# Gated-delta scan: heads in pairs, two pairs half a step apart, with the Fourier output projection as filler

## Chip, cores and metric

One core of one Trainium2 chip. The metric is the device time of one execution in microseconds, lower is better.

## The reference

One encoder layer on 1024 tokens (plus 16 meta tokens) of width 1024, in float32. A combined projection of the normed input gives a Fourier branch, q, k, v of eight heads, an output gate z and two branch gates. Each head runs a gated delta rule in chunks of 64 tokens, once forwards and once backwards; a mixture of experts follows.

```python
def step(state, inp):
    q_c, k_c, u_c, w_c, qk_c, dec_c = inp
    v_new = u_c - einsum("bhcd,bhdv->bhcv", w_c, state)
    o_c = einsum("bhcd,bhdv->bhcv", q_c, state) + einsum("bhcs,bhsv->bhcv", qk_c, v_new)
    state = state * dec_c[..., None, None] + einsum("bhcd,bhcv->bhdv", k_c, v_new)
    return state, o_c
...
o = rms_norm(o_fwd + o_bwd, out_norm_g) * silu(zf)
y_d = o @ w_delta
y_f = real(fft2(f_in)) @ w_fourier
merged = sigmoid(gate_f) * y_f + sigmoid(gate_d) * y_d
return merged @ w_out
```

## The kernel before

Stages follow each other on the core: norm and heads (projections of q, k, v, their convolution, and the inverses of the triangular matrices, on the vector engine in pool `ip`), `middle`, `scan`, `delta` (the product with w_delta), `output`, experts. Matmuls of 128 x 512 are made of three products of high and low parts (`mm3_g`, and L220 in `product`), with the split of the operands in `split` (high part on ScalarE, L860, low part on VectorE, L861).

A gate tile is `project_gate` for one of eight column tiles of a kind (0: z, 1: gate of the Fourier branch, 2: gate of the delta branch): 48 matmuls of 128 x 512 at L220, an activation to `zt` (L1689), and stores to `dz` in DRAM. `middle` computes the Fourier transform, gate kind 1, then `fourier_out` for eight tiles (24 matmuls each by `mm3`, L867, then a product with the gate, `gt`, stored to `dmf`), with three tiles of kind 0 between them (ZB). The other thirteen gate tiles are `filling()`, a generator that `fill(ns)` advances by so many ns of matmuls.

`scan` runs eight heads, 16 steps each, both directions at once: the forward chunk stands in partitions 0 to 63, the backward one in 64 to 127. Two heads are under way at a time, four ticks apart. A `scan_step` has: state (four matmuls, L739), R (VectorE, L741), the scaled q part `so` (L744 on ScalarE for t < 8, L746 on VectorE after), T (L748), vd and vn (ScalarE, L750, L752), dS (two matmuls, L757), S (VectorE, L758), Q (L760), the add to `so` (L761), and from t = 8 the squares. Order on TensorE is that of the code in `scan` (`manual_schedule`); the other engines are ordered by the tile scheduler. Loads of a head (`skq`, `svtok`, `sktok`) go over SP for heads 0 and 1, over POOL for the others, T and Q likewise. `scan_out` and `scan_put` norm a head's output, transpose it (L782), multiply with z and store it to `don` as 512 KB over POOL. The PSUM pools are pmain (3), pds (1), pmisc (1), pproj2 (2). Behind the scan stand the puts left over, the rest of the filler, and `delta`, which loads `don`, `dmf` and `dz`. What `fill` and its constants are:

```python
LEAD = 22e3
FILL = 90e3
SHARE = (0.1, 0.2, 0.1, 0.2, 0.2, 0.2)
```

## Time and profile before

| | us |
|---|---|
| median of 3 runs | 1860.27 (1860.0 to 1862.33) |
| profiled execution | 1857.15 |
| its span | 1855.3 |
| last matmul of `middle` starts | 721.08 |
| first state of the scan | 753.04 |
| last step of the scan, about | 1099 |
| first matmul of `delta` | 1122.13 |

The mean granted clock of the profiled execution is 0.966 of full speed. A row of PE's timeline gives the start of a run of like matmuls, the time until the last of them ends, and their number; since matmuls are pipelined, the distance of two starts tells what a group takes, not its length. One float32 matmul shows as two in the counts of the scan's lines.

### The profile page before, as it was taken

The numbers are of one execution on the slowest core, as the hardware profiler recorded it, in microseconds if no ns is written. First come the engines' busy times: TensorE is split into PE (matmuls) and PEld (weight loads), VectorE is DVE, ScalarE is ACT, GpSimd is POOL, SyncE is SP. The second block draws the span as 40 slices with busy tenths as digits, with TensorE's granted clock in tenths as the row PEclk, the third lists the DMA queues.
The fourth block names the chain that finished last, engine by engine and source line by source line (L and its number), as shares of the span: only waits on it lengthen the run. The fifth ranks groups of instructions, "written<-read, shape, count | busy, mean of one in ns | idle before, by whom it ended". The sixth has DMA issues, their size and how long they took to land. (4 is left out here: it accounts for less than half of the span.)

```text
span 1855.3 us, 26469 instructions
## 1 busy us (share of the span) xinstructions
PE 1730.6 (93%) x10018; PEld 1241.1 (67%) x10018; DVE 1043.3 (56%) x2195; ACT 696.9 (38%) x1539; POOL 188.4 (10%) x297
## 2 busy tenths in 40 slices
PE   7978989889999999799999999999699999999996
PEld 6968888878978887566666677888544443443342
DVE  6645558777955898456556555632634344424433
ACT  5645546444432211444444443421133232323231
POOL 2000001000010001023223100000100111001000
PEclk9998999988999999899999999999899999999998
DMA  4143542334466346734434337735499999999995
GB/s 156 51 124 114 159 137 93 101 105 134 137 198 179 122 158 206 193 106 137 146 114 128 101 117 246 224 98 216 143 402 418 419 419 419 420 419 419 420 419 204
DMA packets 149613, 395.35 MB, mean 213 GB/s; under 512 B 68151, under 2 KB 70367, under 8 KB 124511
## 3 DMA queue, kind: packets, MB, share of 16 engines
q1 hardware_dynamic: 132744, 337.65, 49.3%
q0 software_dynamic: 15248, 55.21, 9.2%
q8 instruction: 81, 1.33, 0.3%
q10 hardware_dynamic: 1488, 0.73, 0.2%
q14 instruction: 52, 0.43, 0.1%
HBM read 330.38 MB, written 65.26 MB: 213 GB/s over the span
## 5 line engine op out<-in xcount | busy, mean ns | idle before, releaser
L220 PE MATMUL proj<-xh,wh 128*128 128x346 f32 (+5 forms) x1080 | 395.9, 367 | 12.1 <-ACT pad L356 6.2
L220 PE MATMUL proj<-xl,wh 128*128 128x346 f32 (+4 forms) x1080 | 395.6, 366 | 0.0
L220 PE MATMUL proj<-xh,wl 128*128 128x346 f32 (+4 forms) x1080 | 394.0, 366 | 0.0
L220 PEld LDWEIGHTS proj<-xh,wh 128*128 128x128 f32 (+1 forms) x1080 | 208.2, 193 | 33.2 <-ACT pad L356 7.0
L220 PEld LDWEIGHTS proj<-xl,wh 128*128 128x128 f32 (+1 forms) x1080 | 208.1, 193 | 18.7 <-issue 5.8
L220 PEld LDWEIGHTS proj<-xh,wl 128*128 128x128 f32 (+1 forms) x1080 | 207.3, 192 | 19.3 <-issue 6.7
L373 DVE SCALAR_TENSOR_TENSOR acc<-pad,convw,acc 128x520 f32<-128x520 f32 x192 | 136.2, 752 | 22.2 <-ACT acc L369 22.1
L860 ACT ACTIVATE wh<-wr 128x1024 fp32r<-128x1024 f32 (+2 forms) x77 | 77.2, 1004 | 132.1 <-PE proj L220 68.2
L1336 DVE SCALAR_TENSOR_TENSOR ea<-ea,gw,gu 128x256 f32<-128x256 f32 x32 | 15.4, 480 | 176.3 <-ACT ea L1335 176.3
L861 DVE TENSOR_TENSOR wl<-wr,wh 128x1024 fp32r<-128x1024 f32 (+2 forms) x77 | 88.8, 1154 | 40.9 <-ACT wh L860 40.7
L688 DVE TENSOR_TENSOR tmp<-M 128x62 f32<-128x62 f32 (+30 forms) x124 | 105.9, 854 | 7.2 <-DMA M<-dL 5.6
L690 DVE TENSOR_TENSOR M<-M,tmp 128x62 f32<-128x62 f32 (+30 forms) x124 | 105.9, 854 | 1.8
L741 DVE SCALAR_TENSOR_TENSOR R<-main,egn,svtok 128x128 f32<-128x128 f32 x128 | 44.8, 350 | 101.6 <-PE main L739 101.5
L750 ACT ACTIVATE vd<-main,vdec 128x128 f32<-128x128 f32 x128 | 46.9, 366 | 137.0 <-PE main L748 136.8
L758 DVE SCALAR_TENSOR_TENSOR S<-S,egl,dS 128x128 f32<-128x128 f32 x240 | 72.6, 342 | 39.5 <-PE dS L757 39.1
L739 PE MATMUL main<-S,skq 128*64 128x128 f32 x1024 | 86.1, 288 | 0.1
L1335 ACT ACTIVATE ea<-gu 128x256 f32<-128x256 f32 x32 | 12.3, 384 | 187.3 <-PE gu L1331 187.3
L1361 DVE TENSOR_TENSOR yl<-dn,yh 128x512 fp32r<-128x512 f32 x64 | 44.1, 689 | 60.1 <-ACT yh L1360 60.1
L739 PEld LDWEIGHTS main<-S,skq 128*64 128x64 f32 x1024 | 54.7, 137 | 31.0 <-DVE so L761 16.9
L1360 ACT ACTIVATE yh<-dn 128x512 fp32r<-128x512 f32 x64 | 38.1, 595 | 97.8 <-PE dn L1358 97.2
L1331 PE MATMUL gu<-ml,gx 128*64 128x512 f32 x288 | 68.7, 594 | 3.0 <-DMA ml<-in_w_gu_dram 3.0
L1331 PE MATMUL gu<-mh,gx 128*64 128x512 f32 x288 | 67.0, 593 | 1.5 <-DMA mh<-in_w_gu_dram 1.5
(430 smaller groups left out, 3161.7 us busy)
## 6 DMA issues: line engine op xcount, KB each, us to landing
mh<-in_w_gu_dram SPq DMA_DIRECT2D x36, 1024.0 KB
ml<-in_w_gu_dram SPq DMA_DIRECT2D x36, 1024.0 KB
wr<-in_w_t_dram SPq DMA_DIRECT2D x52, 512.0 KB
wx<-in_w_gu_dram SPq DMA_DIRECT2D x20, 1024.0 KB
mh<-in_w_dn_dram SPq DMA_DIRECT2D x20, 1024.0 KB
ml<-in_w_dn_dram SPq DMA_DIRECT2D x18, 1024.0 KB
yh<-in_w_gu_dram SPq DMA_DIRECT2D x16, 1024.0 KB
yl<-in_w_gu_dram SPq DMA_DIRECT2D x16, 1024.0 KB
```

What stands on the lines that cost most here:

```text
L220: nc.tensor.matmul(o, w[:, k, :n], x[:, k, a:b], start=(m == 0), stop=(m == 23))
L373: nc.vector.scalar_tensor_tensor(o, pad[:, a + j:a + j + NT // 2], w[:, j:j + 1], o, op0=OP.mult, op1=OP.add)
L688: nc.vector.tensor_tensor(tv, M[:, j + 1:, j:j + 1].to_broadcast([np_, m, j]), M[:, j:j + 1, :j].to_broadcast([np_, m, j]), op=OP.mult)
L690: nc.vector.tensor_tensor(M[:, j + 1:, :j], M[:, j + 1:, :j], tv, op=OP.add)
L739: nc.tensor.matmul(ps[hs[half], i], kv[:, i, 2 * (p % 4) + half], st[half], start=True, stop=True)
L741: nc.vector.scalar_tensor_tensor(R, ps[:, 0], self.egn[:, col:col + 1], d["vtok"][p // 4][:, p % 4], op0=OP.mult, op1=OP.add)
L750: nc.scalar.activation(vd, ps[:, 2], AF.Copy, scale=self.vdec[:, col:col + 1])
L758: nc.vector.scalar_tensor_tensor(st[half], st[half], self.egl[:, half, col:col + 1], dS, op0=OP.mult, op1=OP.add)
L860: self.nc.scalar.activation(hi, src, AF.Copy)
L861: self.nc.vector.tensor_tensor(lo, src, hi.bitcast(F32), op=OP.subtract)
L1331: nc.tensor.matmul(pg[self.HS[i]], d["x"][:, 4 * kk + k, c:c + 64], w[:, 4 * i + k], start=(kk == 0 and k == 0), stop=(kk == 1 and k == 3))
L1361: nc.vector.tensor_tensor(yl[:, cs], pd, yh[:, cs].bitcast(F32), op=OP.subtract)
```

## The change

Heads go in pairs P = 0 to 3, and two pairs (lanes) run half a step apart: in half-step u one lane does its state and its solve (T), the other, of which the step began in the half-step before, its update (dS, S) and its output (Q). PSUM tiles hold two heads; T and Q have a bank each (pTQ), pmain is pM with 2 buffers, the transposes share pproj2 with the filler. For t of 8 and more the scaled q part goes from ScalarE to `oq` and is added on POOL. The output is put in two halves per pair, at t = 11 and t = 15; loads of z and stores of `don` are on SP, 64 stores of 128 KB. T and Q come in blocks of four steps on SP, loads of a pair on SP (first half of the first two pairs) or POOL. All 24 gate tiles stand in `middle`; `fourier_out` is the filler, and its inputs yh, yl, its weights and the scan's right-hand tiles lie where the normed input and the weight tiles were until the middle's end (`hx.close()`).

```diff
-            for _ in self.project_gate(1):
-                pass
-            with tc.tile_pool(name="wf", bufs=2) as tp:
-                yh, yl = self.load_y(tp, self.dy, 4)
-                for dt in range(8):
-                    self.fourier_out(tp, pf, dt, yh, yl)
-                    if dt < self.ZB:
-                        for _ in self.project_gate(0, dt, dt + 1):
-                            pass
+            for kind in (1, 0, 2):
+                for _ in self.project_gate(kind):
+                    pass
...
+        d["o"] = sc.tile([128, 8, 2, 128], F32, name="so", bufs=3)
+        d["ss"] = sc.tile([128, 8, 2], F32, name="oss", bufs=3)
...
+    def pair_load(self, d, b, eng):
+        for i in range(2):
+            h = 2 * d["P"] + i
             ps = slice(4 * b, 4 * b + 4)
+            eng.dma_start(d["kq"][i, b], self.dkq[h][:, :, 512 * b:512 * b + 512])
+            eng.dma_start(d["vtok"][i, b], self.dv[h][:, ps])
+            eng.dma_start(d["ktok"][i, b], self.dk[h][:, ps])
...
+            T, Q = self.slots[d["lane"], i, k % 2]
+            for half in range(2):
+                hs = self.HALVES[half]
+                n0 = 64 * (half ^ v) + 32 * half + 8 * (h % 4) + 4 * b
+                eng.dma_start(T[hs, :, hs], self.dT[h // 4][n0:n0 + 4].rearrange("p s c -> s p c"))
+                eng.dma_start(Q[hs, :, hs], self.dQK[h][hs, v, 4 * b:4 * b + 4])
...
+        ps = self.pM.tile([128, 2, 2, 128], F32, name="main")
+        for i in range(2):
+            kv = d["kq"][i, p // 4].rearrange("c k (s t) -> c k s t", t=64)
+            for j in range(2):
+                for half in range(2):
+                    nc.tensor.matmul(ps[self.HALVES[half], j, i], kv[:, j, 2 * (p % 4) + half],
+                                     d["S"][i][0 if half == v else 1], start=True, stop=True)
+        d["R"] = R = self.sc.tile([128, 2, 128], F32, name="R")
+        for i in range(2):
+            nc.vector.scalar_tensor_tensor(R[:, i], ps[:, 0, i], self.egn[:, cols[i]:cols[i] + 1],
+                                           d["vtok"][i, p // 4][:, p % 4], op0=OP.mult, op1=OP.add)
+        o = d["o"][:, p] if v == 0 else self.sc.tile([128, 2, 128], F32, name="oq")
+        for i in range(2):
+            nc.scalar.activation(o[:, i], ps[:, 1, i], AF.Copy, scale=self.eg[:, cols[i]:cols[i] + 1])
+        if v == 1:
+            nc.gpsimd.tensor_tensor(d["o"][:, p], d["o"][:, p], o, op=OP.add)
...
+        ps = self.pTQ.tile([128, 2, 128], F32, name="psT")
+        for i in range(2):
+            nc.tensor.matmul(ps[:, i], mats[i][0][:, p % 4], d["R"][:, i], start=True, stop=True)
+        d["vd"] = vd = self.sc.tile([128, 2, 128], F32, name="vd")
+        d["vn"] = vn = self.sc.tile([128, 2, 128], F32, name="vn")
+        for o, c in ((vd, self.vdec), (vn, self.beta)):
+            for i in range(2):
+                nc.scalar.activation(o[:, i], ps[:, i], AF.Copy, scale=c[:, cols[i]:cols[i] + 1])
...
+        dS = [self.pds.tile([128, 2, 128], F32, name=f"dS{half}") for half in range(2)]
         for i in range(2):
             for half in range(2):
+                hs = self.HALVES[half]
+                nc.tensor.matmul(dS[half][:, i], d["ktok"][i, p // 4][hs, p % 4], d["vd"][hs, i], start=True, stop=True)
...
+        ps = self.pTQ.tile([128, 2, 128], F32, name="psQ")
+        for i in range(2):
+            nc.tensor.matmul(ps[:, i], mats[i][1][:, p % 4], d["vn"][:, i], start=True, stop=True)
         o = d["o"][:, p]
+        nc.vector.tensor_tensor(o, o, ps, op=OP.add)
+        if v == 1:
+            for i in range(2):
+                sq = self.sc.tile([128, 128], F32, name="osq", bufs=1)
+                nc.scalar.activation(sq, o[:, i], AF.Square, accum_out=d["ss"][:, p, i:i + 1])
...
+    def pair_put(self, d, b, eng):
+        nc, sc, P = self.nc, self.sc, d["P"]
+        ps4 = slice(4 * b, 4 * b + 4)
+        o = d["o"][:, ps4]
+        zs = []
+        for i in range(2):
+            z = sc.tile([128, 8, 64], F32, name="oz")
+            for k, c in ((0, 4 * b), (4, 12 - 4 * b)):
+                nc.sync.dma_start(z[:, k:k + 4].rearrange("p n t -> p (n t)"), self.dz[0, :, 2 * P + i, 64 * c:64 * c + 256])
+            zs.append(z)
+        x = sc.tile([128, 4, 2], F32, name="ox")
+        nc.vector.scalar_tensor_tensor(x, d["ss"][:, ps4], 1.0 / 128.0,
+                                       self.epsq[:, 2 * P:2 * P + 2, ps4].rearrange("c h p -> c p h"), op0=OP.mult, op1=OP.add)
+        r = rsqrt_of(nc, sc, x, [128, 4, 2], "or")
+        eng.tensor_tensor(o, o, r[:, :, :, None].to_broadcast([128, 4, 2, 128]), op=OP.mult)
         yield
+        for i in range(2):
+            yield
+            ps = self.pproj.tile([128, 512], F32, name="proj")
             for j in range(4):
+                nc.tensor.transpose(ps[:, 128 * j:128 * j + 128], o[:, j, i], self.ident)
             pv = ps.rearrange("p (n a t) -> p n a t", a=2, t=64)
+            z = zs[i]
+            for a, zz in ((0, z[:, 0:4]), (1, z[:, 7:3:-1])):
                 nc.vector.scalar_tensor_tensor(zz, pv[:, :, a], self.ong, zz, op0=OP.mult, op1=OP.mult)
+            for k, c in ((0, 4 * b), (4, 12 - 4 * b)):
+                nc.sync.dma_start(self.don[:, 2 * P + i, 64 * c:64 * c + 256], z[:, k:k + 4].rearrange("p n t -> p (n t)"))
...
+        lanes = []
+        for lane in range(2):
+            d = self.pair(lane)
+            self.pair_load(d, 0, nc.sync)
+            self.pair_mats(d, 0, nc.sync)
+            self.pair_start(d)
+            lanes.append(d)
+        yh, yl = self.load_y(self.fin, self.dy, 4)
+        self.filler = self.fourier_out(yh, yl)
+        for d in lanes:
+            self.pair_load(d, 1, nc.gpsimd)
+            self.pair_mats(d, 1, nc.sync)
         self.fill(self.LEAD)
+        nxt, puts = {}, []
+        prev = None
+        for u in range(65):
+            lane, n = u % 2, u // 2
+            now = None
+            if n < 32:
+                t = n % 16
+                if n == 16:
+                    lanes[lane] = nxt.pop(lane)
+                    self.pair_start(lanes[lane])
+                now = lanes[lane], t
+                self.step_state(*now)
+            if prev is not None and prev[1] < 15:
+                self.step_update(*prev)
+            self.fill(self.FILL / 64)
+            if now is not None:
+                self.step_solve(*now)
+            if prev is not None:
+                self.step_out(*prev)
+                d, t = prev
+                if t in (11, 15):
+                    b = 1 if t == 11 else 0
+                    puts.append(self.pair_put(d, b, nc.vector if d["P"] > 1 and b == 0 else nc.gpsimd))
+                if t % 4 == 3:
+                    k = t // 4 + 2
+                    if k < 4:
+                        self.pair_mats(d, k, nc.sync)
+                    elif d["P"] < 2:
+                        if k == 4:
+                            nxt[d["lane"]] = e = self.pair(d["P"] + 2)
+                            self.pair_load(e, 0, nc.gpsimd)
+                        else:
+                            self.pair_load(nxt_of(nxt, lanes, d), 1, nc.gpsimd)
+                        self.pair_mats(nxt_of(nxt, lanes, d), k - 4, nc.sync)
+            for g in list(puts):
+                if next(g, 1):
+                    puts.remove(g)
+            prev = now
+        while puts:
+            self.fill(self.TAIL / 6)
+            for g in list(puts):
+                if next(g, 1):
+                    puts.remove(g)
+        self.fill(1e9)
+    LEAD = 10e3
+    FILL = 26e3
+    TAIL = 6e3
...
-            hx = ExitStack()
+            cx, hx = ExitStack(), ExitStack()
...
             self.middle()
+            hx.close()
             self.pproj = en(tc.tile_pool(name="pproj2", bufs=2, space=PSUM))
-            self.zp = enx(tc.tile_pool(name="zp", bufs=2, side="right"))
-            self.filler = self.filling()
...
-                self.sc = ens(tc.tile_pool(name="sc", bufs=3, side="right"))
-                self.pmisc = ens(tc.tile_pool(name="pmisc", bufs=1, space=PSUM))
+                self.fin = ens(tc.tile_pool(name="fin", bufs=1, side="right"))
+                self.fw = ens(tc.tile_pool(name="fw", bufs=2, side="right"))
+                self.sc = ens(tc.tile_pool(name="sc", bufs=2, side="right"))
...
-                    self.slp = en2(tc.tile_pool(name="sl", bufs=4))
-                    self.pmain = en2(tc.tile_pool(name="pmain", bufs=3, space=PSUM))
+                    self.slp = en2(tc.tile_pool(name="sl", bufs=8))
+                    self.pM = en2(tc.tile_pool(name="pM", bufs=2, space=PSUM))
+                    self.pTQ = en2(tc.tile_pool(name="pTQ", bufs=1, space=PSUM))
                     self.pds = en2(tc.tile_pool(name="pds", bufs=1, space=PSUM))
...
-                    for h in data:
-                        for _ in self.scan_put(h, data[h]):
-                            pass
-                    self.fill(1e9)
                     sx.close()
-                    hx.close()
+                    cx.close()
...
+        yh = tp.tile([128, kt, S], F32R, name="yh")
+        yl = tp.tile([128, kt, S], F32R, name="yl")
...
+    def fourier_out(self, yh, yl):
+        nc, fw = self.nc, self.fw
+        for dt in range(8):
+            wh, wl = (fw.tile([128, 4, 128], F32R, name=n) for n in ("fwh", "fwl"))
+            wr = fw.tile([128, 4, 128], F32, name="fwr")
+            nc.sync.dma_start(wr, self.io["w_fou"][dt])
+            self.split(wh, wl, wr)
+            for c in range(2):
+                ts = slice(512 * c, 512 * c + 512)
+                ps = self.pproj.tile([128, 512], F32, name="proj")
+                g = fw.tile([128, 512], F32, name="gt")
+                nc.sync.dma_start(g, self.dz[1, :, dt, ts])
+                for n, x in enumerate(self.mm3_g(ps, lambda k: wh[:, k], lambda k: wl[:, k],
+                                                 lambda k: yh[:, k, ts], lambda k: yl[:, k, ts], 4)):
+                    if n == 11:
+                        nc.vector.tensor_tensor(g, g, ps, op=OP.mult)
+                        nc.sync.dma_start(self.dmf[:, dt, ts], g)
+                    yield x
```

On PE, a stretch of the steady scan before, one head-step and a bit (proj is the filler; main<-S the state, dS the update, main<-vn the output, main<-R the solve):

```order
L739 MATMUL main<-S_7335,skq 64x128
L739 MATMUL main<-S_7334,skq 64x128
...
L220 MATMUL proj<-xh,wl 128x512
L757 MATMUL dS_8125<-vd,sktok 128x128
L757 MATMUL dS_8128<-vd,sktok 128x128
L760 MATMUL main<-vn,Q_6579 128x128
L220 MATMUL proj<-xh,wh 128x512
L748 MATMUL main<-R,T_6574 128x128
L739 MATMUL main<-S_7572,skq 64x128
```

The same place after, one half-step of two heads:

```order
L750 MATMUL main<-S_7088,skq 64x128
...
L750 MATMUL main<-S_7093,skq 64x128
L781 MATMUL dS_7677<-vd,sktok 128x128
L781 MATMUL dS_7678<-vd,sktok 128x128
...
L920 MATMUL proj<-yl,fwh 128x512
L767 MATMUL psT<-R,m_7052 128x128
L767 MATMUL psT<-R,m_7054 128x128
L793 MATMUL psQ<-vn,m_7056 128x128
```

The filler that stood between state and update, and between output and solve, is gone from there; one place for it is left, ahead of the solve.

On SP after, between the middle and the scan's first steps (yr is the Fourier branch to be split, skq, svtok, sktok the first pair loads; L711 to L713 stand four times):

```order
L1747 DMA dz<-zt 128x512 [waits DMAHW5_49,Activation_49]
L1718 DMA yr<-dy 128x1024 [waits DMAHW6_49,DVE_49,PE_49]
L1727 DMA fwr<-in_w_fou_dram 128x512 [waits DMAHW7_49]
...
L711 DMA skq<-dkq 128x2x512 [waits DMASW7_49,DMASW6_49,DMAHW0_49,DMASW5_49,DMAHW7_49,DMASW1_49,DMASW0_49]
L712 DMA svtok<-dv 128x512
L713 DMA sktok<-dk 128x512 [waits DMAHW1_49]
...
L1718 DMA yr<-dy 128x1024 [waits DMAHW3_49,DVE_49]
...
L1718 DMA yr<-dy 128x1024 [waits DMAHW7_49,DMAHW3_49,DVE_49]
```

Before, SP's row at this place is the first pair load alone:

```order
L1682 DMA dmf<-gt 128x512 [waits DVE_49]
L705 DMA skq<-dkq 128x2x512 [waits DMAHW4_49,DMAHW5_49,DMAHW1_49,DMAHW7_49,DMAHW0_49,PE_49]
L706 DMA svtok<-dv 128x512
L707 DMA sktok<-dk 128x512 [waits DMAHW2_49]
```

The loads of yr have moved to the scan's head, three of the four behind the pair loads.

On POOL after, near the twelfth step of the first pairs (so<-so,oq is the add of L760, or_y the pow, L816 the multiply of 1024 elements):

```order
L713 DMA sktok<-dk 128x512 [waits DMASW7_49,PE_49]
L760 TENSOR_TENSOR so<-so,oq 128x256 [waits Activation_49]
L713 DMA sktok<-dk 128x512 [waits DMASW0_49,PE_49]
L105 TENSOR_TENSOR or_y<-ox,mh 128x8 [waits DVE_49]
...
L816 TENSOR_TENSOR so<-so,or_y 128x1024 [waits DVE_49]
```

Adds, pow and multiplies stand there between loads that wait for PE; POOL had no such adds and multiplies before.

## Rows read from the trace of the kernel before

**Rows 1.** Stretches: from:to, length, busy of PE, PEld, DVE, ACT, POOL, clock, DMA.

```profile
731.00:753.00 22.00, 16.47 (x64) 12.48 (x62) 18.31 (x25) 3.68 (x5) 8.99 (x13) 0.88 0.93 270
...
900.00:950.00 50.00, 49.17 (x375) 33.75 (x375) 30.59 (x103) 22.99 (x78) 17.63 (x27) 1.00 0.49 141
```

**Rows 2.** Timeline of PE at the middle's end: start, us, engine, line, operation, count.

```profile
721.08 0.40 PE L867 MATMUL four<-yh,wl 128*128 128x512 f32 x1
721.31 0.40 PE L220 MATMUL proj<-xh,wh 128*128 128x512 f32 x1
...
739.91 0.39 PE L220 MATMUL proj<-xh,wl 128*128 128x512 f32 x1
```

**Rows 3.** Timeline of PE in the scan, a little more than one head-step.

```profile
900.11 0.66 PE L739 MATMUL main<-S,skq 128*64 128x128 f32 x8
...
902.25 0.47 PE L220 MATMUL proj<-xh,wh 128*128 128x512 f32 x1
902.65 0.66 PE L739 MATMUL main<-S,skq 128*64 128x128 f32 x8
903.24 0.50 PE L220 MATMUL proj<-xl,wh 128*128 128x512 f32 x1
903.67 0.49 PE L757 MATMUL dS<-vd,sktok 64*128 64x128 f32 x4
904.09 0.49 PE L760 MATMUL main<-vn,Q 128*128 128x128 f32 x2
904.33 0.48 PE L220 MATMUL proj<-xh,wl 128*128 128x512 f32 x1
904.65 0.38 PE L748 MATMUL main<-R,T 128*128 128x128 f32 x2
904.96 0.66 PE L739 MATMUL main<-S,skq 128*64 128x128 f32 x8
```

**Rows 4.** Groups by line, 753 to 1099: count, busy, mean ns, idle before.

```profile
L220 PE MATMUL proj<-xh,wl 128*128 128x512 f32 x142 | 66.7, 469 | 0.0
```

**Rows 5.** Timeline of PE behind the scan, one group of transposes.

```profile
1118.43 0.60 PE L782 MATMUL misc<-cst,so 128*128 128x128 f32 x4
1118.79 0.48 PE L220 MATMUL proj<-xl,wh 128*128 128x512 f32 x1
```

**Rows 6.** Timeline of DVE in the step of rows 3.

```profile
903.35 0.35 DVE L741 SCALAR_TENSOR_TENSOR R<-main,egn,svtok 128x128 f32<-128x128 f32 x1 [0.90 <-PE main L739]
...
904.19 0.60 DVE L758 SCALAR_TENSOR_TENSOR S<-S,egl,dS 128x128 f32<-128x128 f32 x2 [0.23 <-PE dS L757]
```

**Rows 7.** Groups by line, 753 to 1099, POOL and DVE.

```profile
L105 POOL TENSOR_TENSOR or_y<-oss,mh 128x8 f32<-128x8 f32 x7 | 11.8, 1684 | 34.3 <-DVE oss L770 34.3
...
L705 POOL DMA_DIRECT2D skq<-dkq x12 | 8.6, 720 | 36.8 <-PE main L739 35.4 <-issue 0.6 <-PE dS L757 0.6
L772 DVE TENSOR_TENSOR so<-so,or_y 128x1024 f32<-128x1024 f32 x7 | 8.6, 1223 | 0.2
...
L709 POOL COPY S<-S 128x128 f32<-128x128 f32 x5 | 1.5, 297 | 0.0
```

**Rows 8.** Timeline of PE at the scan's head; in brackets idle time and its releaser.

```profile
749.33 0.79 PE L220 MATMUL proj<-xh,wh 128*128 128x512 f32 x1 [5.53 <-ACT zt L1689]
...
753.04 1.12 PE L739 MATMUL main<-S,skq 128*64 128x128 f32 x8
```

**Rows 9.** Instructions on tile yr: ns min/median/max, first and last start.

```profile
L860 ACT ACTIVATE yh<-yr x28: 613/632/1064, 633.0 to 1190.4; 128x512 fp32r<-128x512 f32 x24, 128x1024 fp32r<-128x1024 f32 x4
L861 DVE TENSOR_TENSOR yl<-yr,yh x28: 681/692/1226, 634.3 to 1191.0; 128x512 fp32r<-128x512 f32 x24, 128x1024 fp32r<-128x1024 f32 x4
...
L1668 SPq DMA_DIRECT2D yr<-dy x4: 319/349/424, 629.0 to 637.8; - x4
```

**Rows 10.** Line L220 on PE by stretch: length, busy, count, clock, DMA.

```profile
721.30:753.00 31.70, 26.16 (x104) 0.92 0.86 262
1099.00:1122.00 23.00, 22.61 (x97) 1.00 0.71 242
```

200 lines of the change are left out of this document (52 added, 148 removed).

## Prediction

> **What bounds the kernel now.** The table by stretch comes first. In the scan (753 to 1099 us) PE is busy for nearly all of a stretch at the granted clock of 1.00, the 2.4 GHz level, while the vector engine stands at 61% and DMA at 0.49 [rows 1]. So before hides the scan's data waits behind PE, and PE's own order of short matmuls is the bound. The PE timeline shows what these cost. A dense run of 512-column matmuls starts one every 0.2325 us (80 starts from 721.31 to 739.91) [rows 2]. One head-step, from 900.11 to 902.65, takes 2.54 us with three fillers in it [rows 3]; without them 2.54 − 3 × 0.2325 = 1.84 us. In it a change between the 64-wide forms (state, dS) and the 128-wide ones costs extra: the filler ahead of the state lasts 0.40 instead of 0.23, the one ahead of dS 0.43, so 0.17 to 0.20 us for each change [rows 3]. The scan's filler, 142 of each of three kinds [rows 4], takes 426 × 0.2325 = 99 of the 346 us, and 14 groups of four transposes at 0.36 [rows 5] take 5; what is left is 242 us for 128 head-steps, 1.89 each, close to the 1.84 of the undisturbed one.
>
> **Moved filler.** All 24 gate tiles now stand in the middle, where thirteen more, 13 × 48 = 624 matmuls, run at the dense pitch, and the 192 matmuls of fourier_out leave it: +145.1 − 44.6 = +100.5 us there, and as much less behind it. The pitch is the same for both kinds, 0.23 on either side of the seam at 721.31 [rows 2]. Sum 0. The splits, evictions and stores of a gate tile I cost at nothing: they hide behind its own 48 × 0.2325 = 11.2 us of matmuls, as they do in the dense run; if that cover were gone, a tile would wait for its weights' split, about 1.2 us by the row of an equally large operation on DVE [rows 7].
>
> **Pairs.** Now eight state matmuls stand together, then four dS, one or two fillers, two T, two Q. From one head-step [rows 3]: state 0.59 for the first head and 0.59 − 0.16 for the second, which needs no change of form, 1.02; dS 0.42 and 0.21 more, 0.63; what the last filler ahead of a T takes over its pitch (0.32 instead of 0.23), 0.09; T and Q at 0.21 a head (0.24 from Q to the filler behind it is the upper bound), 0.86; the way back into the state form 0.10. Sum 2.70 us a half-step of two heads, against 2 × 1.89. 64 × 2.70 = 172.8 us in place of 242: **−69 us**. Sixteen groups of transposes stay sixteen. With 0.2 more for changes of form, 2.9, it is −56; if the second heads cost as little as a second T, 2.5, it is −82.
>
> **The lane's own chain.** It has two half-steps, 2 × (2.70 + 1.94 × 0.2325) = 6.3 us (124 fillers by the order), for state, R, T, vd, dS, S. R starts 0.70 after the state [rows 3, 6]; for two heads R ends at about 1.5 us of a half-step, where PE asks for it at 2.2. S starts 0.52 after dS [rows 3, 6], and four S (two take 0.60) end some 2.7 us into the half-step, where the next state is due at 3.16. It fits with 0.4 us to spare, as long as nothing else stands on DVE there. What does stand there: 16 multiplies of gt and 8 splits of fwl, 0.69 each by the split's row [rows 9]. Each can push S 0.3 us past its time: 24 × 0.3 = +7.
>
> **The output of a pair.** It comes in halves, eight in all: add, square, pow on POOL (1.68 [rows 7]), four short DVE operations, and the multiply of 1024 elements, on POOL in six of the eight; the transposes that need it stand two half-steps, 6.3 us, later in PE's fixed order. POOL's queue holds, in order, the adds of L760, 24 loads of the next pairs (0.72 to issue a large one, and waiting until PE has freed the buffers [rows 7]) and these multiplies. The nearest rows for a multiply on POOL are DVE's own, 1.22, and POOL's copy, 0.30 for 128 elements, eight of which make 2.4 [rows 7]; I take 2.4, the only one of POOL. With 1.22 a put's chain is about 5.5 us and fits its 6.3; with 2.4 and a wait for the queue it doesn't. I put ten places (six multiplies, four bursts of six loads) at 1.1 us each: +11 (0 if all fit; 40 at 4 us each). Waits in the scan together: **+18 us** (0 to 47). The Trainium skill ("GPSIMD Engine Reference", 4.1 Engine selection) speaks against this part: it gives elementwise work on a tile to VectorE and calls GPSIMD about twice slower for two inputs. No row of before shows a two-input multiply on POOL; by the page it is an estimated 2 × 1.22 = 2.4 us, and the sum would stay; by DVE's row alone the six multiplies would be 6 × 1.2 = 7 us cheaper.
>
> **The head of the scan.** Before, 31.7 us lie between the middle's end at 721.31 and the first state at 753.04 [rows 2, 8], with 104 fillers (24.2 us) in them [rows 10]; 7.5 us are lost, 5.53 of them in one wait [rows 8], and the granted clock of the last 22 us is 0.88 [rows 1]. Those fillers needed nothing that wasn't loaded. The new ones need yh and yl, whose memory is free only after the last gate, and yr is single: its first load stands ahead of the 12 pair loads (4 MB) in SP's queue, the other three behind them. At this stretch's 270 GB/s [rows 1] 4 MB take 15 us. A yr before was split 4.0 us after its issue (629.0 to 633.0), and the two halves of a split of 1024 are 1.06 and 1.23 [rows 9]. So the first is split about 6 us after the last gate, the second lands behind the pair loads at about 22, and two more rounds of 4.0 + 2.3 follow: the last k stands at about 22 + 2.3 + 2 × 6.3 = 37. Of the 47 lead fillers (10.9 us) some 5 us are then left: first state about 41 us after the last gate, 30 of them not filler, against 7.5. The mats loads and memsets lie beside that. **+24 us** (10, if the yr loads get through beside the pair loads, to 33, if all of it runs one after another or at the lower clock).
>
> **The tail.** Before, 97 fillers [rows 10] cover the last head's put and the loads of delta. After, about 20 fillers (4.7 us) and four groups of transposes are left, and the last put (pow 1.68, short operations, multiply 1.22 on DVE, transposes, store and load at about 4 each, split) takes some 15 us before delta's last k is there; delta's first k cover about 4 of that: **+6 us** (0 to 12).
>
> **Sum.** 0 − 69 + 18 + 24 + 6 = −21 us. The profiled execution took 1857.15 and becomes 1836; the median of before, 1860.27, lies 3.1 above it, so I forecast **1839 us**.
>
> **Rivals.**
> (a) *Every wait in the scan is hidden.* The slack of 0.4 us and DVE at 61% [rows 1] speak for it, POOL's queue against. −69 + 0 + 10 + 0 = −59: 1801. Chance 0.20.
> (b) *POOL becomes the bound; slower.* Place: steps 8 to 15 of each pair, where POOL's add of oq stands between ACT and DVE's add of psQ, and the other lane's R queues behind that add on DVE. The loads of before already wait for PE on POOL, 35.4 us in 12 of one kind [rows 7]; there nothing hangs on the queue, here such a load has an add behind it that the scan needs. Ten places at 6 us are 60, not 11: −69 + 67 + 24 + 6 = +28, 1888. It decides from ten places at 3.2 us (11 + 21). Against it: eight buffers of each kind are free for the most part when these loads are issued. Chance 0.22.
> (c) *Pairing doesn't share the changes of form*, and a half-step is two old head-steps, 3.78 us. Then the −69 is 0 and the sum +48: 1908. Against it: Q is followed by a filler 0.24 later, no change paid [rows 3]. Chance 0.05.
> (d) *The yr loads get through early*, the rest as forecast: head +10, 1825, inside the forecast's own range.
>
> **How the numbers follow.** The forecast, with (d), 0.48 (1812 to 1866), (a) 0.20 (1796 to 1812), (b) 0.22 (1866 to 1905), (c) 0.05, still faster 0.05. A measurement of this kernel can tell about 0.2%, 3.7 us, from no change. Faster by more: (a), the rest below it and 0.36 of the forecast, 0.61. Within 0.2%: 0.10, the forecast's upper part. Slower: 0.02 of the forecast, (b) and (c), 0.29. The range leaves out what is below 1798, (c) and the upper half of (b), 2 in 10: 1798 to 1882; the forecast's own is 1812 to 1866.
>
> **What would show it.** On PE's timeline: dS directly behind the state of the other lane, half-steps of 3.2 us, and from first to last step about 172.8 + 124 × 0.2325 + 12 × 0.36 + 18 = 224 us. PE waiting in front of transposes for POOL's multiply confirms the put term; a wait in front of fillers for yh or yl behind the last gate the head; waits of T for R, with DVE standing on POOL's add, are rival (b). I am wrong if half-steps of 2.70 plus fillers don't appear (c), or if a middle with 24 gates runs slower than 0.2325 a matmul.

## The result and the profile after

| | before | after |
|---|---|---|
| median (lowest to highest, 4 runs each) | 1860.13 (1858.12 to 1862.33) | 1889.23 (1886.62 to 1890.38) |
| profiled execution, its span | 1857.15, 1855.3 | 1890.38, 1888.6 |
| last matmul of the middle starts | 721.08 | 822.85 |
| first state of the scan | 753.04 | 882.06 |
| last Q, about | 1099 | 1122.03 |
| first matmul of delta | 1122.13 | 1148.07 |

The ratio is 1.0154, with an interval of 1.0137 to 1.0172: the change makes the kernel slower by 1.5%. I had forecast 1839 and a range of 1798 to 1882; the time lies above the range and on the other side of no change.

The page's first part after: busy time, share of the span, instructions of each engine.

```profile
span 1888.6 us, 26727 instructions
PE 1686.7 (89%) x10018; PEld 1247.7 (66%) x10018; DVE 1018.7 (54%) x2062; ACT 709.8 (38%) x1603; POOL 175.5 (9%) x264
```

Which wait ends last is told stage by stage. The table by stretch after (from:to, length, busy PE, PEld, DVE, ACT, POOL with counts, granted clock, DMA share, GB/s):

```profile
823.00:882.00 59.00, 17.50 (x49) 10.79 (x47) 8.95 (x10) 6.60 (x8) 11.17 (x28) 0.60 0.70 242
900.00:950.00 50.00, 50.00 (x538) 42.25 (x536) 35.19 (x113) 30.85 (x111) 3.62 (x5) 1.00 0.30 81
950.00:1000.00 50.00, 38.50 (x359) 31.71 (x357) 29.85 (x92) 25.99 (x104) 27.11 (x35) 0.90 0.65 190
1122.50:1148.00 25.50, 12.33 (x39) 8.89 (x39) 14.14 (x30) 6.92 (x14) 4.10 (x4) 0.61 0.88 316
```

The second row, the undisturbed scan, is what the pairing was to bring: PE busy throughout, 538 matmuls in 50 us where [rows 1] have 375. The other three are seams: the head of the scan, the first outputs of pairs, and the tail. There PE stands, and the granted clock falls with it: in the head and the tail it is 0.60 and 0.61, nearer the 1.2 than the 2.4 GHz level. PE's waits from 820 to 1150 after (who waits for whom; us, times, longest) name what ends them:

```profile
PE proj L920 <- ACT yh L913: 33.6, 3, 26.5
PE proj L822 <- POOL so L816: 11.0, 4, 4.2
PE proj L822 <- DVE oz L826: 8.6, 4, 4.7
PE psT L767 <- DVE R L754: 6.9, 2, 4.6
PE proj L920 <- ACT fwh L913: 6.5, 1, 6.5
PE proj L822 <- DVE so L816: 6.0, 1, 6.0
```

L920 is the filler, L822 the transposes of a pair's output, L767 a T. With the prices of a filler (0.2325) and of a group of transposes (0.36, [rows 5]) taken off, the profiled executions differ as follows. "Lost" is time with neither of these nor a half-step's own work in it.

| term | forecast | measured | how |
|---|---|---|---|
| gates to the middle | 0 | +1 | last gate expected at 721.08 + 100.5 = 821.6, stands at 822.85 |
| pairs | −69 | −65 | half-step without fillers 2.76 instead of 2.70; 64 × 2.76 = 177 for 242 |
| lost in the scan | +18 | +30 | 240.0 − 177 − 124 × 0.2325 − 12 × 0.36 |
| lost in the head | +24 | +41 | 59.2 − 47 × 0.2325 = 48.3, before 7.5 |
| lost in the tail | +6 | +19 | 26.0 − 21 × 0.2325 − 4 × 0.36 = 19.7, before about 0.4 |
| sum, by delta's first matmul | −21 | +26 | 1122.13 to 1148.07 |

Delta and the experts add little: PE's last matmul is 26.5 later, delta's first 25.9. The span grew by 33.3, so another 6.7 lie behind the last work, in a step that I had not thought of (last section).

### The profile page after: what moved, and what is told of

It is laid out like the page before. It is cut to its first block, busy times and chain, and to the rows that moved or that the text cites. A ratio compares the mean times of both kernels' runs of the same rounds, so it can differ in the third digit from the quotient of the medians.

```text
span 1888.6 us, 26727 instructions
## 1 busy us (share of the span) xinstructions
PE 1686.7 (89%) x10018; PEld 1247.7 (66%) x10018; DVE 1018.7 (54%) x2062; ACT 709.8 (38%) x1603; POOL 175.5 (9%) x264
## 4 chain that ended last, share of the span: by engine, by line
PE 48%; DMA 33%; DVE 9%; ACT 3%; issue 2%; SPq 2%; POOL 1%; DVEq 0%; ACTq 0%; POOLq 0%
PE proj L224 16%; PE proj L920 11%; DMA F<-dF 6%; PE gu L1384 4%; DMA ml<-in_w_gu_dram 4%; PE main L750 3%; DVE acc L377 3%; DMA mh<-in_w_dn_dram 2%; DMA mh<-in_w_gu_dram 2%; DMA wx<-in_w_gu_dram 2%; DMA yl<-in_w_gu_dram 2%; DMA yh<-in_w_gu_dram 2%; PE dn L1411 2%; PE dS L781 2%; PE four L610 2%
## 5 line engine op out<-in xcount | busy, mean ns | idle before, releaser
L224 PE MATMUL proj<-xh,wh 128*128 128x346 f32 (+5 forms) x1080 | 384.0, 356 | 5.8 <-ACT pad L360 4.6
L224 PE MATMUL proj<-xl,wh 128*128 128x346 f32 (+4 forms) x1080 | 383.4, 355 | 0.0
L224 PE MATMUL proj<-xh,wl 128*128 128x346 f32 (+4 forms) x1080 | 381.7, 354 | 0.0
L224 PEld LDWEIGHTS proj<-xh,wh 128*128 128x128 f32 (+1 forms) x1080 | 206.6, 191 | 27.4 <-ACT pad L360 5.8
L224 PEld LDWEIGHTS proj<-xl,wh 128*128 128x128 f32 (+1 forms) x1080 | 206.0, 191 | 18.8 <-issue 0.6
L224 PEld LDWEIGHTS proj<-xh,wl 128*128 128x128 f32 (+1 forms) x1080 | 205.9, 191 | 18.2 <-issue 0.2
L377 DVE SCALAR_TENSOR_TENSOR acc<-pad,convw,acc 128x520 f32<-128x520 f32 x192 | 136.2, 752 | 22.2 <-ACT acc L373 22.2
L914 DVE TENSOR_TENSOR wl<-wr,wh 128x1024 fp32r<-128x1024 f32 (+1 forms) x69 | 83.3, 1209 | 99.7 <-ACT wh L913 97.4
L913 ACT ACTIVATE wh<-wr 128x1024 fp32r<-128x1024 f32 (+1 forms) x69 | 72.2, 1048 | 138.3 <-PE proj L224 109.0
L750 PE MATMUL main<-S,skq 128*64 128x128 f32 x1024 | 72.4, 285 | 0.0
L785 DVE SCALAR_TENSOR_TENSOR S<-S,egl,dS 128x128 f32<-128x128 f32 x240 | 67.3, 342 | 2.3 <-PE dS L781 1.2
L920 PE MATMUL proj<-yh,fwh 128*128 128x512 f32 x64 | 30.9, 483 | 40.1 <-ACT yh L913 33.6
L914 DVE TENSOR_TENSOR yl<-yr,yh 128x512 fp32r<-128x512 f32 (+1 forms) x28 | 21.2, 766 | 77.5 <-ACT yh L913 77.5
```

The costliest lines, as they stand in the source:

```text
L224: nc.tensor.matmul(o, w[:, k, :n], x[:, k, a:b], start=(m == 0), stop=(m == 23))
L377: nc.vector.scalar_tensor_tensor(o, pad[:, a + j:a + j + NT // 2], w[:, j:j + 1], o, op0=OP.mult, op1=OP.add)
L750: nc.tensor.matmul(ps[self.HALVES[half], j, i], kv[:, j, 2 * (p % 4) + half], d["S"][i][0 if half == v else 1], start=True, stop=True)
L785: nc.vector.scalar_tensor_tensor(S, S, self.egl[:, half, cols[i]:cols[i] + 1], dS[half][:, i], op0=OP.mult, op1=OP.add)
L913: self.nc.scalar.activation(hi, src, AF.Copy)
L914: self.nc.vector.tensor_tensor(lo, src, hi.bitcast(F32), op=OP.subtract)
```

## Experiments

Each kernel is the changed one with the edit shown, which is shortened. Times of e2 to e9 are single profiled executions, those of e10 to e13 medians of four with a ratio to the kernel before. The kernel before took 1861.62 beside e2 to e4 and 1854.65 beside e5 to e8, so whole times of these two groups compare only to some 7 us; the lengths of the stages are the safer measure. "Head" is from the last gate matmul to the first state (in e12 and e13 to the second, as the first stands among the gates there), "scan" from there to the last Q, "tail" to delta's first matmul.

| kernel | time | last gate | head | scan | tail |
|---|---|---|---|---|---|
| after | 1890.38 | 822.85 | 59.2 | 240.0 | 26.0 |
| e2 multiply on DVE | 1885.73 | 819.44 | 59.4 | 238.3 | 26.4 |
| e3 y loaded first | 1871.44 | 820.19 | 24.1 | 258.4 | 27.3 |
| e4 half the filler | 1891.17 | 818.57 | 58.5 | 228.5 | 48.2 |
| e5 loads under the gates | 1892.08 | 839.29 | 42.1 | 244.4 | 21.2 |
| e6 transposes later | 1887.12 | 820.03 | 60.2 | 235.6 | 28.0 |
| e7 = e3, four z buffers | 1852.48 | 819.29 | 24.8 | 248.3 | 20.4 |
| e8 = e5, e6, e7 | 1866.39 | 841.81 | 24.0 | 238.5 | 19.6 |
| e9 = e7, second loads later | 1852.42 | 818.32 | 24.3 | 250.9 | 20.4 |
| e10 = e9, e6, first loads on POOL | 1847.9 | 818.63 | 24.7 | 242.2 | 19.8 |
| e11 = e10, states first | 1837.08 | 820.3 | 8.6 | 239.4 | 19.0 |
| e12 = e11, S early | 1826.77 | 824.42 | 1.5 | 236.6 | 21.2 |
| e13 = e12, 48 more loads on POOL | 1844.64 | 847.17 | 1.5 | 237.6 | 21.9 |

Three theories were to be told apart: that the head's loss is the loads of y in the queue; that the loss at the puts is POOL's multiply; and, as a rival to the second, that it is the length of the put's whole chain, its z buffers among it.

### The head: e3

```diff
-        yh, yl = self.load_y(...)          # behind the pair loads, one yr at a time
+        for k in range(4):                 # ahead of the pair loads
+            nc.sync.dma_start(yl[:, k].bitcast(F32), self.dy[:, k])
+        for k in range(4):
+            self.split(yh[:, k], yl[:, k], yl[:, k].bitcast(F32))
```

> The four loads of the Fourier branch go straight into yl, which is split in place (no single yr buffer), and stand ahead of the pair loads. Theory A (the fillers wait for yr, each of which waits for the buffer and stands behind the pair loads): the first state comes 25 to 35 us after the last gate matmul instead of 58.9, the time falls by 22 to 30 us, to about 1863. Rival B (the 8 MB of pair loads on two queues set the head by themselves): the first state waits for them, 45 us or more after the last gate, and the time falls by 5 to 12 us.

The head fell from 59.2 to 24.1, so the loads of y are what made it long: their place in the queue and their single buffer together, since the edit changes both (e5 below moves pair loads alone). But only 19 us came off the total: PE's timeline of e3 (start, us, line, tile, and what the idle time before it waited for) has the missing 17 in the very first half-step.

```profile
844.25 1.09 PE L750 MATMUL main<-S,skq 128*64 128x128 f32 x16
845.28 0.50 PE L920 MATMUL proj<-yh,fwl 128*128 128x512 f32 x1
862.79 0.76 PE L920 MATMUL proj<-yh,fwh 128*128 128x512 f32 x1 [17.01 <-DVE gt L1747]
863.36 1.05 PE L767 MATMUL psT<-R,m 128*128 128x128 f32 x4
```

The filler's PSUM tile waits for the product with gt, and the filler's own next loads stand on SP behind twelve pair loads: the weight load fwr issued at 837.95 landed at 854.8, and the load of gt was issued behind it, at 858.92. The 47 lead fillers had eaten what was loaded; the stage's loads of 8 MB still stood ahead of the rest.

### The puts: e2, e6, e4

```diff
-  puts.append(self.pair_put(d, b, nc.vector if d["P"] > 1 and b == 0 else nc.gpsimd))
+  puts.append(self.pair_put(d, b, nc.vector))
```

> All eight multiplies of a put are on DVE (six were on POOL). If POOL's multiply and its queue make PE wait (11.0 us in four waits of the transposes for POOL's so), these waits fall to 4 us or less together and the time falls by 5 to 8 us, to about 1883. If the length of the whole chain add, square, pow, short operations, multiply is the cause, the waits come back as waits for DVE's so and the time stays within 2 us of 1889.

PE's longest waits from the first state to the last Q, first of after, then of e2:

```profile
PE proj L822 <- POOL so L816: 11.0, 4, 4.2
PE psT L767 <- DVE R L754: 6.9, 2, 4.6
PE proj L822 <- DVE oz L826: 2.1, 2, 1.1
```

```profile
PE psT L767 <- DVE R L754: 7.7, 3, 4.7
PE proj L822 <- DVE so L816: 5.5, 3, 2.8
PE proj L822 <- DVE oz L826: 4.2, 3, 2.1
```

The multiply takes 1.22 on DVE and 1.90 on POOL, and the wait for it in the scan falls by half, from 11.0 to 5.5 us. (Over head, scan and tail DVE's so is 10.9 in e2, but 5.4 of this is the tail's, which was 6.0 in after.) But the waits for oz and R behind it grow, and the scan is only 1.7 us shorter. So POOL's price is about half of this wait, and with two z buffers hardly any time is won by it; the other half is the chain in front of the transposes, too long for two half-steps with either engine.

```diff
-        yield
+        for _ in range(3 if b else 1):   # the transposes of b = 1 two half-steps later
+            yield
```

> The transposes of the puts at t = 11 stand two half-steps (6.4 us) later in PE's order, nothing else moves. Theory A (the chain add, square, pow, short operations, multiply is longer than the two half-steps it has): the waits of these transposes for POOL's so (4.0 us in the first cluster, 0.8 and 2.0 in the third) go, 5 to 9 us less, about 1882; the wait for oz stays, since it hangs on a buffer. Rival B (POOL or DVE can't keep up with two puts): the waits come back two half-steps later, at most 2 us less.

The first half-step of the first put fell from 10.27 to 5.19 us, as a chain that is given more time should. But the wait of T for R grew from 4.6 to 6.3, and the scan is only 4.4 shorter. So a second cause stands behind the first, and e7 names it.

```diff
-    FILL = 26e3
+    FILL = 13e3
```

> The filler in the scan is halved (FILL 13e3): about 62 matmuls of 0.2325 us move from the half-steps behind the last one. If PE's order sets the half-step and the lane's chain has 0.4 us to spare, most half-steps become 2.99 us (scan 14 us shorter), and the 14 us of filler cover the tail's waits: 8 to 14 us less in all, about 1878. If the chain sets the half-step, it stays near 3.2 us, the scan keeps its length and the time stays or rises by up to 4 us.

With one filler a half-step takes 2.99 instead of 3.22, exactly a filler less: the lanes' own chain has slack. In after, too, no half-step outside the clusters of puts is longer than 3.22, though DVE's gt and fwl stand in some of them. The scan is 11.5 shorter for 62 fillers less (14.4), and the tail 22.2 longer, 0.36 for each filler there. So filler is worth most inside the scan, and the lost time of the scan isn't filler's.

### The z buffers: e7, and what they explain

Four buffers of z instead of two have no room in the changed kernel alone (e1: the pair tiles want 72 KB a partition, 69.4 would be left). They need the memory that yr holds, so they come on top of e3.

```diff
-                z = sc.tile([128, 8, 64], F32, name="oz")
+                z = sc.tile([128, 8, 64], F32, name="oz", bufs=4)
```

> As e3_y_first, and the z tiles of the puts have four buffers instead of two (the room comes from yr). Against e3_y_first (1871.4): if z loads that wait for a store to leave their buffer hold up DVE, R and T, the 4.5 us and 1.7 us waits of T for R and the tail's 4.4 us for oz go, 8 to 14 us less, about 1860. If POOL's multiply is the whole of the put stalls, at most 3 us less, 1868 or more.

Against e3 the scan is 10.1 shorter (0.8 of it in the first half-step), the tail 6.9, and delta's first matmul comes 17.2 earlier (the time is 19.0 less). The timelines of after show why; first DVE, then SP, then PE, at the second half of the first put.

```profile
983.85 0.88 DVE L826 SCALAR_TENSOR_TENSOR oz<-proj,ong,oz 128x256 f32<-128x256 f32 x2 [6.45 <-DMA oz<-dz]
984.64 0.60 DVE L754 SCALAR_TENSOR_TENSOR R<-main,egn,svtok 128x128 f32<-128x128 f32 x2
...
976.96 0.86 SPq L828 DMA_DIRECT2D don<-oz  x2
981.71 0.80 SPq L810 DMA_DIRECT2D oz<-dz  x2
...
985.13 1.20 PE L767 MATMUL psT<-R,m 128*128 128x128 f32 x4 [4.63 <-DVE R L754]
```

A put of two heads takes both z buffers. The other lane's put, one half-step later, can load its z only when the first one's stores have ended (store at 976.96, load at 981.71). DVE stands 6.45 us for that load, and R of the scan, which has all it needs, stands behind it in DVE's queue: PE's T waits 4.63 for a step of which no wait shows in R's own row. e7 has no wait of a T for R left among its longest.

### The loads under the gates: e5, e8, e9

```diff
-                    d[name][i, b] = sl.tile(shape, F32, name="s" + name)
+                    d[name][i, b] = (self.sla if (P // 2 + b) % 2 == 0 else sl).tile(...)
...
+            with self.tc.high_priority(offset=100000):   # first loads in a pool of their own, early
+                self.pair_load(d, 0, nc.sync)
+                self.pair_mats(d, 0, nc.sync)
```

> The first half of the pair loads (4 MB on SP) gets a pool of its own in memory that is free before the middle's end, so these loads run under the gates; the rest as in the changed kernel, yr single and its loads serial. If the 8 MB of pair loads between the yr loads made the head long (second yr 17.5 us after its issue), each yr round takes about 6.3 us, the first state comes some 35 us after the last gate (59 before) and the time falls by 18 to 26 us, to about 1867. If the single yr buffer alone made it, the head stays over 50 us and the time falls by at most 8.

The edit moved more than the text above says: the clearing of the matrices' tiles and the loads of both halves' matrices went early with it. POOL's second 4 MB did not: their memory comes free only with the last gate, and they are issued from 846.86 on. The second yr was there 13.4 us after the last gate instead of 34.5, and the head fell to 42.1, not to 35, with the single yr and POOL's loads still in it. And nothing was gained: the last gate came 16.4 later. PE's waits in the middle of e5, and SP's timeline there:

```profile
PE proj L224 <- ACT zt L1750: 18.1, 1, 18.1
...
628.34 0.55 SPq L711 DMA_DIRECT2D skq<-dkq  x1
...
661.19 1.02 SPq L1751 DMA_DIRECT2D dz<-zt  x2
```

The loads and 16 pairs of loads of matrices hold SP from 628 to 661, the gate's store dz stands behind them, its tile zt is not free, and the gates' own matmuls wait 18.1 for it. A load moved ahead is paid by what stands behind it on its queue.

```diff
+        yh, yl = self.load_y4(self.fin, self.dy, 4)    # e3
+                z = sc.tile([128, 8, 64], F32, name="oz", bufs=4)    # e7
+            for _ in range(3 if b else 1):    # e6
+            with self.tc.high_priority(offset=100000):    # e5
```

> Early first pair loads, the Fourier branch split in place, four z buffers and late transposes at t = 11 together. If head, z buffers and put chain are separate losses, they add: head 59 to about 20 us with no stall of the first fillers behind it (38 less), z buffers 10, late transposes 6, so 1889 - 54 = 1835, faster than before the change (1860). If the gains overlap or a stall moves to another place, about 1850.

e8 puts these together and misses both expected times, 1835 and 1850: head, scan and tail are 0.8, 9.8 and 0.8 shorter than e7's, the last gate 22.5 later; 13.9 slower in all. Of the scan's 9.8, 7.9 are the first half-step (19.30 to 11.38), which the early loads bring, and only 2 the clusters of puts: with later transposes the first cluster (half-steps 25 to 29) gives 6.3 back, and the other two take 4.1 of it again. On SP the early loads cost more than the scan gives.

```diff
-        for d in lanes:                    # ahead of the lead
-            self.pair_load(d, 1, nc.gpsimd)
...
+            if u < 2:                      # behind the filler of half-steps 0 and 1
+                self.pair_load(lanes[u], 1, nc.sync)
+                self.pair_mats(lanes[u], 1, nc.sync)
```

> As e7_y_oz4 (1852.5), and the second half of the first pair loads (4 MB) goes from POOL, where it starts with the first half, to SP behind the first steps. If the 8 MB at the head delay the weight and gate loads of the filler (fwr landed 17 us after its issue and the first half-step waited 16 us for DVE's gt), the first half-step falls from 19.3 to under 8 us and the time by 8 to 16 us, to about 1841. If the filler's loads wait for their own buffers instead, the first half-step stays near 19 us and the time within 3 us of 1852.

e9 changed nothing (1852.42 for 1852.48): the first half-step still took 18.9. But this doesn't clear the 4 MB, for they didn't go behind the filler's loads. SP's timeline of e9:

```profile
836.48 0.52 SPq L711 DMA_DIRECT2D skq<-dkq  x1
...
847.75 0.32 SPq L713 DMA_DIRECT2D sktok<-dk  x1
848.47 0.33 SPq L1737 DMA_DIRECT2D fwr<-in_w_fou_dram  x1
...
855.67 0.80 SPq L1743 DMA_DIRECT2D gt<-dz  x2
```

The twelve second loads stand on SP from 836.48 to 847.75, still ahead of the filler's next weights (848.47) and of the gt (855.67) that ends PE's wait; they changed their queue and not their place. So e9 alone doesn't decide between its two theories, but four runs side by side do. With 8 MB of pair loads at the head, the half-step takes 19.3 (e7, 4 on SP and 4 on POOL) and 18.9 (e9, all on SP); with 4 MB there and 4 under the gates, it takes 11.4, whether the 4 are on POOL (e8) or on SP (e10 below). It goes by the bytes at the head and not by their queue; what the remaining 8 us of wait are made of stays open.

### Together: e10, e11, e12

```diff
+            with self.tc.high_priority(offset=100000):
+                self.pair_load(d, 0, nc.gpsimd)
+            self.pair_mats(d, 0, nc.sync)
```

> As e9_defer, with the first half of the pair loads on POOL under the gates (in e5_two_pools they stood on SP ahead of the gates' weight loads and the middle ended 17 to 20 us later) and the transposes of t = 11 two half-steps later. If the head is a matter of what is under way on the DMA queues when the middle ends, the middle ends at 820 again, the first half-steps are free of waits and the time is 1830 to 1838, faster than before the change by over 1%. If the loads delay the middle from POOL too, the end of the gates moves to 830 or later and the time is 1845 or more.

e10 adds to e9 the transposes of e6 and the second pool of e5, its first loads on POOL, which has little to do under the gates. The middle's end stays (818.63) and the first half-step falls from 18.9 to 11.4, as in e8; that is 7.6 of the scan's 8.7. It isn't free of waits, as the better of the two expected cases had it: 8.3 us of it are still one for gt. 1847.9 (1843.45 to 1851.43) against 1862.4: ratio 0.9922 (0.9898 to 0.9946).

```diff
-    LEAD = 10e3
+    LEAD = 0
...
-            self.fill(self.FILL / 64)
+            if u >= 8:                     # no filler before the ninth half-step
+                self.fill(640)
```

> As e10_best, with no filler ahead of the first state and none in the first eight half-steps; behind them three fillers a half-step instead of two. If the head's loss is that the new filler's inputs are late (10 us wait for the first split, 8 us for gt), the states start without it: first state 6 to 14 us after the last gate instead of 24.7, no 8 us stall in the first half-step, and the time falls from 1848 by 10 to 20 us, to about 1833. If memory that is freed only at the middle's end sets the head whatever the filler, the first state stays over 20 us behind the last gate, and the time is 1845 or more.

With the pairs' data loaded under the gates, the scan can begin without the filler's. The head is 8.6, of which 8.20 are one wait:

```profile
828.88 2.11 PE L750 MATMUL main<-S,skq 128*64 128x128 f32 x16 [8.20 <-POOL S L720]
```

1837.08 (1833.76 to 1842.64), ratio 0.9883 (0.9858 to 0.9907). What is left is the copy of the first state S, whose memory still came free with the last gate. e12 moves it to the early pool:

```diff
-  S = [self.slp.tile([128, 128], F32, name=f"S{j}", bufs=8) for j in range(2)]
+  S = [self.sla.tile([128, 128], F32, name=f"S{j}", bufs=8) for j in range(2)]
```

> As e11_state_first, with the state tiles S in the early pool, so that they are written before the middle's end; the first states then stand among the last gate tiles on PE. If only the memory of S holds the first state, it starts ahead of the middle's end, and the time is 3 to 10 us under e11_state_first, about 1827. If R, vd and the other tiles of the scan, which lie where the normed input was, hold the steps anyway, the waits fall among the gates, and the time is equal to e11_state_first or above it.

PE's timeline of e12 at the seam (L224 is the gate's matmul; the matmuls of the first state stand among the gates from 660.36 to 707.26, over 117 us ahead of the last one, and the state at 825.93 is the second):

```profile
707.10 0.43 PE L750 MATMUL main<-S,skq 128*64 128x128 f32 x2
...
824.42 0.39 PE L224 MATMUL proj<-xh,wl 128*128 128x512 f32 x1
825.25 0.75 PE L767 MATMUL psT<-R,m 128*128 128x128 f32 x4 [0.44 <-DVE R L754]
825.93 1.09 PE L750 MATMUL main<-S,skq 128*64 128x128 f32 x16
```

and its scan as one stretch:

```profile
824.00:1062.50 238.50, 223.48 (x2220) 185.97 (x2219) 167.32 (x511) 141.89 (x518) 59.09 (x68) 0.99 0.53 162
```

The seam is gone, and the granted clock of the scan is 0.99. e12 takes 1826.77 (1824.7 to 1828.45) against 1859.3: ratio 0.9814 (0.9794 to 0.9835), faster than the kernel before by 1.9%, and 62 us below the median of the changed one. In its scan, counted from the second state (1.8 us of the 177 lie ahead of it), 236.6 − 175 − 172 × 0.2325 − 12 × 0.36 = 17 us are still lost, the longest wait 4.8 for a multiply on POOL, and 15 in the tail, 7.5 of them in one wait for the last multiply.

## Why the prediction was wrong, point by point

The profiled execution was to take 1836 and took 1890.38. Of the 54 us between them 17 are the head's, 13 the tail's, 12 the scan's, 7 the program's closing, 4 the pairs' and 1 the gates'. The step that failed is the pricing of transfers: the head's sum left out 4 MB that POOL loads, and the z loads of a put, which wait for the stores ahead of them, stood in the scan and the tail at nothing.

**Right.** The bound and the pairing. The half-step stands on PE's timeline after as it was put together from [rows 3]:

```profile
954.70 1.09 PE L750 MATMUL main<-S,skq 128*64 128x128 f32 x16
955.73 0.72 PE L781 MATMUL dS<-vd,sktok 64*128 64x128 f32 x8
956.37 0.50 PE L920 MATMUL proj<-yl,fwh 128*128 128x512 f32 x1
956.71 0.39 PE L920 MATMUL proj<-yh,fwl 128*128 128x512 f32 x1
956.94 0.61 PE L767 MATMUL psT<-R,m 128*128 128x128 f32 x4
957.38 0.61 PE L793 MATMUL psQ<-vn,m 128*128 128x128 f32 x4
957.92 1.09 PE L750 MATMUL main<-S,skq 128*64 128x128 f32 x16
```

State 1.03, dS 0.64, two fillers 0.57, T 0.44, Q 0.54: 3.22. I had 1.02, 0.63, the fillers with 0.09 over their pitch, 0.86 for T and Q and 0.10 for the way back. Rival (c) is out. The moved gates at 0 were right within 1.3 us.

**The lane's own chain, +7.** Wrong, and too high: undisturbed half-steps take 3.22 whether or not gt and fwl stand in them, and e4 shows the chain fits even into 2.99. The loss was 0.

**The output of a pair, +11, measured +30.** The step that failed here is the choice of the mechanism. I worked out the price of the multiply and of POOL's queue, and costed the z loads and their store at nothing, though the change itself shows `oz` in a pool of two, two tiles a put, and two puts half a step apart. PE's timeline after has nine long half-steps (10.27, 6.69, 9.86; 9.80, 6.41, 6.13; 4.66, 6.37, 5.20) in three clusters, not ten small waits. PE's waits in the scan are 22.6 of the 30. Behind them the granted clock falls: from 971 to 974 it is 0.50, the 1.2 GHz level, and a state takes 1.90 there instead of 1.03. I had no term for that. The multiply is 1.90 rather than 2.4; e2 shows that its engine is half of the wait for it, but 1.7 us of the scan as long as z has two buffers. Of the loss, the buffers are about 9 by e7 against e3, the distance to the transposes 2 to 4 (e8 against e7, e6 against after). The chain's remaining links are not separated, above all a wait for the multiply in the second cluster: 4.2 to 4.8 in the kernels with this one on POOL, 2.8 in e2. No run put the multiplies on DVE together with four z buffers, and none gave the transposes of t = 15 more time. Here the Trainium skill ("GPSIMD Engine Reference", 4.1 Engine selection), which calls GPSIMD about twice slower for two inputs, is borne out in direction: 1.90 against 1.22 is 1.55 times. But its advice to keep the multiply off GPSIMD was worth only these 1.7 us in e2.

**The head, +24, measured +41.** Right in kind, mis-sized at two places. These rows of after, of SP, POOL and then ACT, show the first:

```profile
823.27 0.32 SPq L1718 DMA_DIRECT2D yr<-dy  x1
829.61 0.55 SPq L711 DMA_DIRECT2D skq<-dkq  x1
839.84 0.32 SPq L1718 DMA_DIRECT2D yr<-dy  x1
859.73 6.36 SPq L1718 DMA_DIRECT2D yr<-dy  x2
...
834.12 2.96 POOL L711 DMA_DIRECT2D skq<-dkq  x4
...
857.39 1.06 ACT L913 ACTIVATE yh<-yr 128x1024 fp32r<-128x1024 f32 x1 [25.35 <-DMA yr<-dy]
863.43 1.06 ACT L913 ACTIVATE yh<-yr 128x1024 fp32r<-128x1024 f32 x1 [4.99 <-DMA yr<-dy]
```

I put the second yr at 22 us behind the last gate, behind the 4 MB of SP. It was split at 34.5: POOL issued the pairs' second 4 MB from 834.12 on, 3 of them ahead of the yr of 839.84, and I had left these out of the sum. They landed in turn with SP's, SP's last at 856.14, POOL's last at 857.06, and the yr at 857.36. The two rounds behind it took 6.0 each, as forecast (6.3). The second place is the filler itself: its products run through k in order, so only 9 of the 47 lead fillers can run before the last k is there, and 38 were left, 11.5 us at the clock they found (0.78 from 870 to 882), not "some 5". 47.7 + 11.5 = 59.2. My own sum was also 1.4 off: 41 − 10.9 − 7.5 is 22.6 and not 24. Moreover the term had a second half that e3 uncovered: the filler's next loads, 17 us in the first half-step if the head is cured alone.

**The tail, +6, measured +19.** The put's chain was right in kind: PE waits 6.00 for its multiply before the first group of transposes, 0.72 for gt before the second and 1.70 for DVE before the third. Only the 4.75 before the fourth are a z load behind stores, for which DVE stands 5.89; the four are 13.2 together. And I had reckoned fillers and transposes at full clock, where the granted one was 0.50 from 1130 to 1148: 16 of the 21 fillers at 0.42 and four groups at 0.75 are 4.6 more. Two buffers more (e7) took 6.9 off it.

**The rivals.** The time is that of (b), 1888, but (b) did not happen. POOL's add takes 0.73 (32 of them, 23.8 us), half-steps with it last 3.22 like those without, and the two T that wait for R wait for DVE's z load. A rival's price is no proof of its mechanism. The chances themselves leaned the wrong way because the three seams were added as independent small terms, though one thing has a part in all of them, loads that need what the stage before or the put before frees: 25.35 us of ACT's for yr in the head, 6.45 and 3.65 of DVE's for z in the scan, 5.89 in the tail.

**Not foreseen, +6.7.** See the last section.

## What to carry to other kernels

Work that is moved into a gap as filler brings its loads, its buffers and its order with it: at a stage's head count the bytes of every queue that wait for the memory freed there, and begin with the work whose inputs can be loaded under the stage before (in e12 the second state follows the last gate by 1.5 us, where the first one of the changed kernel followed by 59.2). Where two lanes run the same steps half a step apart, each buffer of a load, change and store round is needed for both at once, and with too few, work that needs none of it stands behind the wait (here R of the scan behind DVE's 6.45 us for z). Look for a wait in the row ahead of the late one, not in the late row.

## What the runs showed of the hardware that I had not expected

POOL closes the program, and its closing takes longer after than before. POOL's last rows of before and of after:

```profile
1847.82 0.92 POOL L1401 DMA_INDIRECT out_dram<-G,oidx  x1 [0.44 <-ACTq L1453]
```

```profile
1874.36 0.92 POOL L1454 DMA_INDIRECT out_dram<-G,oidx  x1 [0.44 <-DVEq L1506]
```

From there to the span's end it is 7.5 us before (1855.3) and 14.2 after (1888.6). In the instruction records a closing drain of POOL takes 2.44 and 7.83 of that, and a semaphore step behind it 0.77 and 2.10. Before issues 167 DMAs from POOL, after 95. Over the runs: 167 give 2.44 and 0.77, 95 always 7.83 and 2.10, 83 (e9) 6.85 and 1.86. Was the number the cause? e13 loads 48 times from POOL into a tile that nobody reads, early in the program (from 38 to 75 us):

```diff
+            with tc.high_priority(offset=-3000):
+                for i in range(48):
+                    nc.gpsimd.dma_start(dmy[:, 8 * i:8 * i + 8], io["norm2_t"])
```

> As e12_state_first_S (1826.8), plus 48 loads of 4 KB on POOL in the heads stage, whose data nobody uses. At the program's end POOL's last two steps (a semaphore increase and a drain) took 0.8 and 2.4 us with 167 software DMAs recorded in the kernel before, 2.1 and 7.8 with 95 in the changed one, 1.9 and 6.8 with 83 in e9_defer. If they cost about 0.1 us for each software DMA since a count that wraps between 95 and 167 (167 - 29 = 138), 143 DMAs leave 5 and the two steps take under 1.5 us: 8 to 9 us less, about 1818. If they grow with the count alone, they take 14 to 15 us and the time rises by 4 to 5 us, to 1831.

With 143 the drain was 3.50 and the step 1.02, and the end 8.8 us instead of e12's 14.2. So 48 more of these DMAs take 5.4 us off the end. But 83 close faster than 95, so the end doesn't only fall with their number, and the 143 gave neither of the two cases that I had expected. What the drain counts is open. The loads were no gain: e13 took 1844.64 (1843.49 to 1848.82), ratio 0.9926 (0.9899 to 0.9954), since the last gate came 22.8 later. On the way PE waits 30.8 us in 4 for one tile instead of 5.4 in 1, from 390 us on and so long after the loads had landed; by what the loads bring this about isn't shown.

```profile
PE proj L224 <- ACT pad L360: 30.8, 4, 14.3
```

```profile
PE proj L224 <- ACT pad L360: 5.4, 1, 5.4
```

The first row is e13's, PE's waits from 300 to 848, the second e12's from 300 to 820.
